# A dense gate matrix built with one 64-column matmul per token, the two halves of each gate added by VectorE, in one ring of 40 rows

## The chip, the cores and the metric

One core of one Trainium2 chip. The metric is the device time of one execution in microseconds; lower is better. The core has five engines that each run their own instructions in order: TensorE (PE; its weight loads are listed apart as PEld), VectorE (DVE), ScalarE (ACT), GpSimd (POOL) and SyncE (SP). They wait for each other with semaphores. Matmuls write into PSUM, which has banks of 128 x 512 float32; everything else lies in SBUF.

## The reference

The program is a trunk of two layers on 512 tokens of 1024 features. Layer 0 mixes tokens by windowed attention, layer 1 by a short gated convolution; each is followed by the same kind of expert layer, and that one takes nearly all the time:

```python
def peer_ffn(xn, w_query, sub_keys, expert_u, expert_v):
    q = (xt @ w_query).reshape(T, PEER_HEADS, 2, QUERY_HALF)
    s = jnp.einsum('thpd,hpnd->thpn', q, sub_keys)
    s_top, i_top = lax.top_k(s, PEER_TOPK)
    ...
    g_s, sel = lax.top_k(cand, PEER_TOPK)
    idx = jnp.take_along_axis(cand_idx, sel, axis=-1)
    g = jax.nn.softmax(g_s, axis=-1)
    ...
        u = jnp.take(expert_u, ic, axis=0)
        a = jnp.einsum('td,thkd->thk', xc, u)
        w = gc * jax.nn.gelu(a, approximate=False)
        v = jnp.take(expert_v, ic, axis=0)
        return jnp.einsum('thk,thkd->td', w, v)
```

So each token picks 8 x 16 = 128 experts out of 128 x 128 = 16384, each with a gate g. An expert is a row u and a row v of 1024 numbers; the token gets the sum of g * gelu(x . u) * v over its experts. An expert's number is 128 i + j, where i and j are its two keys.

## The kernel before

**Two ways for the tokens.** The 512 tokens are four tiles of 128. Tiles 0 and 1 are done by `gather` (L625): for each tile, 128 indirect loads fetch a row of u for each token (`ug`, L636, issued on GpSimd), and VectorE takes its dot product with the token (L639, a "dot" below, followed by a short read of the accumulator). Later 128 rows of v each are fetched (`vg`, L667) and multiplied on TensorE in pairs, eight matmuls of 512 columns to a pair (`acc`, L677).

Tiles 2 and 3, 256 tokens, are done by `dense` (L693): all 16384 experts are computed for all of them, and a gate matrix G that is zero almost everywhere picks. The loop runs over the 128 key blocks i, each with the 128 experts j. Its two halves are:

- `ustep(i)` (L704): the block of u is loaded, split into a rounded part (`uh`, cast on ScalarE, L701) and a remainder (`ul`, subtracted on VectorE, L702), and multiplied with the tokens in 24 matmuls of 256 columns into the bank psA (L178 to L183). ScalarE puts the gelu of it into `dw` (L712).
- `vstep(i)` (L715): `dw` is multiplied with the row of G for block i (L718; on VectorE, or on GpSimd while the gather's dots run), split into `wh` (ScalarE, L724) and `wl` (VectorE, L725); the block of v is split like u (`vh`, `vl`); 12 matmuls of 512 columns add to y (L736), which holds four banks from the first block to the last. `ustep` runs seven blocks ahead of `vstep` (LAG), and the first eight blocks' `dw` lie in a G tile not yet needed (`pre`).

**The gate matrix.** G[j, i, token] is the gate of expert (i, j). `gen(i, tg)` (L739) makes it for 32 blocks (a chunk) and 16 tokens (a group). VectorE builds three things in float16: `oj`, one where j is the expert's second key (128 x 2048, L745), `oi`, one where i is its first (128 x 512, L748), and two copies of `oi` times the gate, rounded and remainder (L751, twice; the gate is scaled by GSC). TensorE multiplies `oj` with them, for each token two matmuls of 32 columns that accumulate in the bank psG (L756, 32 matmuls in all). ScalarE scales the bank into four G tiles of eight rows each (L759). There are five such tiles, so 40 rows in flight. A layer has 4 chunks of 16 groups: 128 groups in the program. psG has one bank, which it shares by turns with other small products; psA has one as well.

**The order.** The code of `dense`, of the gather and of the next layer's front (mixer, router) is written as streams that a planner (`merge`) interleaves by estimated prices; in the loop, two groups for the next chunk are written before each vstep from the 25th of a chunk on (L782 to L787). The tile framework then schedules by simulated times; groups have a high priority (HPG), so they are taken as soon as their buffers and inputs are there. What comes out is a fixed order on each engine.

## Time and profile before

| | us |
|---|---|
| median of 3 runs | 3108.2 (3102.3 to 3110.3) |
| profiled execution, its own time | 3084.04 |
| its span, first to last instruction | 3082.2 |
| mean granted TensorE clock | 0.950 |
| dense loop of layer 0, first y matmul to the last chunk's end | 665 to 1670 |
| dense loop of layer 1 | 2117 to 3082 |

The chances in the prediction are about the median. The profile is of one execution, which was 0.8% under it. In the profile "busy" is the time in which an engine executes; matmuls are pipelined, so a TensorE that is busy all the time need not be at its peak. In the tables of windows each line is one stretch of the span: its length, then busy time and number of instructions of TensorE, its weight loads, VectorE, ScalarE and GpSimd, then the granted clock of TensorE as a share of 2.4 GHz, the share of the DMA engines in use, and the rate in GB/s.

### The profile page before, as it was taken

What the parts mean: (1) busy time and instruction counts of PE and PEld (TensorE: products, weight loads), DVE (VectorE), ACT (ScalarE), POOL (GpSimd) and SP (SyncE); (2) the same over time, 40 slices, a digit from 0 to 9 for tenths busy, and PEclk for the clock granted to TensorE, in tenths of its full rate; (3) what the DMA queues carried; (4) which work ended last, traced back from release to release, by engine and by line L of the source; (5) the groups of instructions that cost most, each with busy time, mean ns of one, the idle gap of its engine ahead of it and who ended that gap; (6) DMA issues with size and microseconds to landing.
All of it is one profiled execution on the core that took longest, in us unless ns stands there. A gap on an engine that the chain in (4) does not pass through costs nothing.

```text
span 3082.2 us, 53493 instructions
## 1 busy us (share of the span) xinstructions
PE 2782.4 (90%) x19980; PEld 2242.6 (73%) x19980; DVE 2255.1 (73%) x5363; ACT 1178.1 (38%) x2414; POOL 1352.1 (44%) x1154
## 2 busy tenths in 40 slices
PE   5964799999998999999997798999998798999998
PEld 5862367757986887778776787775787687778776
DVE  2499859887996997455459998887479999456444
ACT  4225433424333334344343334333434333334433
POOL 0157643354354444531347752345326866531331
PEclk8986899979999999999999899997999999999999
DMA  5888888879889977985999996787959988975996
GB/s 193 299 312 307 323 303 292 307 278 359 299 329 381 356 268 260 328 301 178 350 335 387 373 359 220 264 306 270 319 193 377 357 297 321 340 274 182 341 338 215
DMA packets 263205, 931.40 MB, mean 302 GB/s; under 512 B 29984, under 2 KB 38560, under 8 KB 262944
## 3 DMA queue, kind: packets, MB, share of 16 engines
q0 software_dynamic: 147456, 536.94, 48.1%
q1 hardware_dynamic: 115488, 391.03, 35.2%
q8 instruction: 158, 2.59, 0.3%
q14 instruction: 103, 0.84, 0.1%
HBM read 916.31 MB, written 11.53 MB: 301 GB/s over the span
## 4 chain that ended last, share of the span: by engine, by line
PE 72%; DVE 14%; DMA 5%; issue 4%; ACT 3%; POOL 1%; SPq 0%; DVEq 0%; ACTq 0%; POOLq 0%
PE y L736 20%; PE acc L677 9%; PE psG L756 9%; PE psA L180 8%; PE psA L181 7%; PE psA L183 7%; DVE ug L639 7%; PE psrq L568 3%; DMA ug<-in_u_dram,idx 2%; PE psbcu L404 1%; DMA vg<-in_v_dram,idxT 1%; PE psq L241 1%; DVE vl L702 1%; PE psrs L574 1%; PE psrq L180 1%
## 5 line engine op out<-in xcount | busy, mean ns | idle before, releaser
L667 POOL DMA_INDIRECT vg<-in_v_dram,idxT x512 | 550.0, 1074 | 945.7 <-PE acc L677 839.0
L636 POOL DMA_INDIRECT ug<-in_u_dram,idx x512 | 670.3, 1309 | 626.5 <-DVE act L639 269.8
L639 DVE CUSTOM_DVE_ANT_0 ug<-ug,xn 128x1024 f32<-128x1024 f32 x512 | 628.8, 1240 | 27.5 <-DMA ug<-in_u_dram,idx 26.7
L180 PE MATMUL psA<-xh,uh 128*128 128x256 f32 x2048 | 525.5, 294 | 44.7 <-ACT uh L701 26.8
L702 DVE TENSOR_TENSOR ul<-du,uh 128x1024 fp32r<-128x1024 f32 x256 | 316.4, 1236 | 264.5 <-ACT uh L701 244.9
L181 PE MATMUL psA<-xl,uh 128*128 128x256 f32 x2048 | 503.7, 284 | 0.0
L180 PEld LDWEIGHTS psA<-xh,uh 128*128 128x128 f32 x2048 | 391.9, 191 | 147.6 <-ACT wh L724 54.5
L702 DVE TENSOR_TENSOR vl<-dv,vh 128x1024 fp32r<-128x1024 f32 x256 | 319.9, 1249 | 183.5 <-ACT vh L701 169.4
L701 ACT CAST uh<-du 128x1024 fp32r<-128x1024 f32 x256 | 269.5, 1053 | 340.7 <-PE psA L181 296.4
L181 PEld LDWEIGHTS psA<-xl,uh 128*128 128x128 f32 x2048 | 391.5, 191 | 5.3 <-issue 3.0
L701 ACT CAST vh<-dv 128x1024 fp32r<-128x1024 f32 x256 | 268.8, 1051 | 240.8 <-PE y L736 198.3
L677 PE MATMUL acc<-vg,wd 128*32 128x512 f32 x2048 | 315.8, 637 | 10.4 <-DMA vg<-in_v_dram,idxT 10.0
L756 PEld LDWEIGHTS <-oj 128*128 128x128 f16 x4096 | 278.1, 159 | 63.1 <-issue 37.6
L736 PE MATMUL y<-vh,wh 128*128 128x512 f32 x1024 | 291.5, 404 | 26.6 <-ACT vh L701 26.6
L756 PE MATMUL psG<-oi,oj 128*128 128x32 f16 x4096 | 298.4, 249 | 7.6 <-ACT G L759 6.6
L183 PE MATMUL psA<-xh,ul 128*128 128x256 f32 x2048 | 292.2, 284 | 5.3 <-DVE ul L702 5.3
L736 PE MATMUL y<-vl,wh 128*128 128x512 f32 x1024 | 281.7, 397 | 11.6 <-DVE vl L702 11.6
L183 PEld LDWEIGHTS psA<-xh,ul 128*128 128x128 f32 x2048 | 264.4, 190 | 23.5 <-issue 9.2
L736 PE MATMUL y<-vh,wl 128*128 128x512 f32 x1024 | 278.7, 394 | 0.0
L759 ACT ACTIVATE G<-psG 128x128 f32<-128x128 f32 x512 | 102.5, 282 | 366.5 <-PE psG L756 346.2
L745 DVE TENSOR_TENSOR oj<-ijT,iorep 128x2048 f16<-128x2048 f16 x128 | 157.8, 1233 | 108.9 <-PE psG L756 108.6
L736 PEld LDWEIGHTS y<-vh,wh 128*128 128x128 f32 x1024 | 181.1, 192 | 71.4 <-ACT vh L701 35.1
(207 smaller groups left out, 3902.6 us busy)
## 6 DMA issues: line engine op xcount, KB each, us to landing
du<-in_uT_dram SPq DMA_DIRECT2D x256, 512.0 KB, 6.2
dv<-in_v_dram SPq DMA_DIRECT2D x256, 512.0 KB, 6.2
wpc<-in_wq_dram SPq DMA_DIRECT2D x64, 512.0 KB, 5.7
wpc<-in_w_in_dram SPq DMA_DIRECT2D x48, 512.0 KB, 6.7
wpo<-in_wo_dram SPq DMA_DIRECT2D x16, 512.0 KB, 4.5
ug<-in_u_dram,idx POOLq DMA_INDIRECT x512, 7.3
vg<-in_v_dram,idxT POOLq DMA_INDIRECT x512, 6.9
wpo<-in_w_out_dram SPq DMA_DIRECT2D x16, 512.0 KB, 7.3
```

The lines of the kernel that those rows point to most:

```text
L180: nc.tensor.matmul(ps, w[0][:, k, :], x[0][:, k, ts], start=(k == 0), stop=False)
L181: nc.tensor.matmul(ps, w[0][:, k, :], x[1][:, k, ts], start=False, stop=False)
L183: nc.tensor.matmul(ps, w[1][:, k, :], x[0][:, k, ts], start=False, stop=(k == KC - 1))
L636: nc.gpsimd.indirect_dma_start(out=ug, out_offset=None, in_=a[f"u{l}"], in_offset=bass.IndirectOffsetOnAxis(ap=r["idx"][h][:, c:c + 1], ax ...
L639: nc.vector.tensor_tensor_reduce(out=ug, in0=ug, in1=xn, scale=1.0, scalar=0.0, op0=ALU.mult, op1=ALU.add, accum_out=act[:, s:s + 1])
L667: ld = nc.gpsimd.indirect_dma_start(out=vg, out_offset=None, in_=a[f"v{l}"], in_offset=bass.IndirectOffsetOnAxis(ap=idxT[:, tt:tt + 1], ax ...
L677: mm = nc.tensor.matmul(acc[c:c + 32, :], wd[:, j, r8, :], vgs[j][:, h * 512:(h + 1) * 512], start=(q == 0 and r8 == 0), stop=(q == 3 and ...
L701: nc.scalar.copy(hi, w)
L702: nc.vector.tensor_tensor(lo, w, hi, op=ALU.subtract)
L736: nc.tensor.matmul(ys[tt][h], x[:, tt * P:(tt + 1) * P], m[:, h * 512:(h + 1) * 512], start=first and k == 0, stop=last and k == len(terms ...
L745: nc.vector.tensor_tensor(oj, jT.unsqueeze(1).to_broadcast([P, P, TG]), iorep, op=ALU.is_equal)
L756: nc.tensor.matmul(ps[:, T * IC:(T + 1) * IC], oj[:, :, T], oi[:, q, :, T], start=(q == 0), stop=(q == 1))
```

## The change

Three things are changed together, all in `dense`:

- The rounded gate and the remainder of one token are no longer two matmuls that accumulate. One matmul of 64 columns puts them side by side in psG. A bank then holds 8 tokens (TP) instead of 16, so each group has two parts of 8 matmuls.
- ScalarE scales the rounded half into G, and VectorE then adds the scaled remainder, read from PSUM (`scalar_tensor_tensor`, a new instruction).
- G is one tile, a ring of 40 rows (GR), in place of five tiles of 8 rows. The 32 rows of a chunk begin at row 0, 32, 24 or 16; where they run over the ring's end, both the scaling and the addition are split in two (8+24, 16+16 and 24+8 rows). The first eight `dw` lie in rows 32 to 39.

```diff
-HC = 8
+TP = 8
...
-GB = 5
+GR = 40
...
-            w = (pre[:, i, :] if i < npre else
+            w = (G[:, IC + i, :] if i < npre else
...
-            (nc.gpsimd if (WPU if st.get("gu") else WPV) else nc.vector).tensor_tensor(w, w, G[i // HC][:, i % HC, :], op=ALU.mult)
+            (nc.gpsimd if (WPU if st.get("gu") else WPV) else nc.vector).tensor_tensor(w, w, G[:, i % GR, :], op=ALU.mult)
...
-            ps = pmm("psG")
-            for T in range(TG):
-                for q in range(2):
-                    nc.tensor.matmul(ps[:, T * IC:(T + 1) * IC], oj[:, :, T], oi[:, q, :, T],
-                                     start=(q == 0), stop=(q == 1))
-            for hf in range(IC // HC):
-                nc.scalar.mul(G[i // HC + hf][:, :, tg * TG:(tg + 1) * TG],
-                              ps.rearrange("p (t i) -> p i t", i=IC)[:, hf * HC:(hf + 1) * HC, :], 1.0 / GSC)
+            for part in range(TG // TP):
+                ps = pmm("psG")
+                for T in range(TP):
+                    nc.tensor.matmul(ps[:, T * 2 * IC:(T + 1) * 2 * IC].rearrange("p (q i) -> p q i", q=2),
+                                     oj[:, :, part * TP + T], oi[:, 0:2, :, part * TP + T], start=True, stop=True)
+                psv = ps.rearrange("p (t q i) -> p q i t", q=2, i=IC)
+                tok = slice(tg * TG + part * TP, tg * TG + (part + 1) * TP)
+                r0 = i % GR
+                cut = min(IC, GR - r0)
+                for o, n, row in ((0, cut, r0), (cut, IC - cut, 0)):
+                    if n:
+                        g = G[:, row:row + n, tok]
+                        nc.scalar.mul(g, psv[:, 0, o:o + n, :], 1.0 / GSC)
+                        nc.vector.scalar_tensor_tensor(g, psv[:, 1, o:o + n, :], 1.0 / GSC, g,
+                                                       op0=ALU.mult, op1=ALU.add)
...
-        G = {}
+        G = pool.tile([P, GR, T2], F32, name="G")
...
-            if tg == 0:
-                for hf in range(IC // HC):
-                    G[c * (IC // HC) + hf] = pool.tile([P, HC, T2], F32, name="G", tag="G", bufs=GB)
...
-        npre = HC * PRE
-        pre = pool.tile([P, HC, T2], F32, name="pre", tag="G", bufs=GB) if PRE else None
+        npre = GR - IC
```

In numbers: 2048 matmuls in place of 4096 for G, 448 scalings in place of 512, and 448 new additions on VectorE. In the code after, the lines of `gen` are one lower up to the matmul (`oj` L744, `oi` L747 and L750, psG L755), the scaling is L764, the addition L765; ustep and vstep are one lower too.

The change also moves instructions. The places are the last chunk's gate matrix in layer 1 and the one of layer 0.

VectorE in layer 1, where the groups for the last chunk are made. Before, one group's `oj` and `oi` stand between the subtractions of a step:

```order
L725 TENSOR_TENSOR wl<-dw,wh 128x256
L745 TENSOR_TENSOR oj<-ijT,iorep 128x2048
L748 TENSOR_TENSOR oi<-ijT,iorep 128x512
L751 TENSOR_TENSOR oi<-oi,gb 128x512 x2
L702 TENSOR_TENSOR ul<-du,uh 128x1024
L718 TENSOR_TENSOR dw<-dw,G 128x256
L702 TENSOR_TENSOR vl<-dv,vh 128x1024
```

After, this piece of VectorE's order is part of a block in which it repeats about ten times with nothing of a step between:

```order
L744 TENSOR_TENSOR oj<-ijT,iorep 128x2048
L747 TENSOR_TENSOR oi<-ijT,iorep 128x512
L765 SCALAR_TENSOR_TENSOR G<-psG,G 128x24x8
L750 TENSOR_TENSOR oi<-oi,gb 128x512 x2
L765 SCALAR_TENSOR_TENSOR G<-psG,G 128x8x8
L765 SCALAR_TENSOR_TENSOR G<-psG,G 128x24x8
L765 SCALAR_TENSOR_TENSOR G<-psG,G 128x8x8
L744 TENSOR_TENSOR oj<-ijT,iorep 128x2048
```

The first two additions belong to the group before, part one; the next two to its part two. The `ul`, `dw`, `vl` and `wl` rows that stood between the groups stand before and behind the block.

ScalarE at the same place, before (the scalings of a group are four instructions, and the casts of the steps lie between):

```order
L759 ACTIVATE G<-psG 128x8x16 x4
L701 CAST uh<-du 128x1024
L712 ACTIVATE dw<-psA 128x256
L759 ACTIVATE G<-psG 128x8x16 x4
L701 CAST vh<-dv 128x1024
L724 CAST wh<-dw 128x256
```

and after, at the beginning of the block:

```order
L700 CAST vh<-dv 128x1024
L711 ACTIVATE dw<-psA 128x256
L764 ACTIVATE G<-psG 128x24x8
L764 ACTIVATE G<-psG 128x8x8
L764 ACTIVATE G<-psG 128x24x8
L764 ACTIVATE G<-psG 128x8x8
L764 ACTIVATE G<-psG 128x24x8
```

Over thirty scalings follow each other there; the next cast stands behind them. On TensorE the matmuls of 22 parts stand there behind each other in the same way, ahead of the last four vsteps of the chunk.

VectorE in layer 0 at the step to its last chunk, before (one step's work repeats; `wd` is a copy for the gather):

```order
L660 COPY wd<-wT 128x2x8
L702 TENSOR_TENSOR vl<-dv,vh 128x1024
L725 TENSOR_TENSOR wl<-dw,wh 128x256
L702 TENSOR_TENSOR ul<-du,uh 128x1024
L718 TENSOR_TENSOR dw<-dw,G 128x256
L702 TENSOR_TENSOR vl<-dv,vh 128x1024
L725 TENSOR_TENSOR wl<-dw,wh 128x256
```

After, the end of the block there, in which the gather's dots (two rows each, the second reads the accumulator) stand between the additions:

```order
L765 SCALAR_TENSOR_TENSOR G<-psG,G 128x24x8
L638 ISA ug,act<-ug,xn 128x1024
L638 ISA act 128x1
L638 ISA ug,act<-ug,xn 128x1024
L638 ISA act 128x1
L750 TENSOR_TENSOR oi<-oi,gb 128x512 x2
L765 SCALAR_TENSOR_TENSOR G<-psG,G 128x8x8
L638 ISA ug,act<-ug,xn 128x1024
L638 ISA act 128x1
L765 SCALAR_TENSOR_TENSOR G<-psG,G 128x24x8
L765 SCALAR_TENSOR_TENSOR G<-psG,G 128x8x8
```

Dots and gate parts that were spread over the steps have moved into this block, 67 dots in all.

Counted by vsteps (y groups of 12 matmuls on TensorE, `wl` on VectorE), the order holds this. A stretch is named by its first and last vstep, layer 1 going on from 128; gates are groups of 16 tokens before and parts of 8 tokens after, pairs are the gather's on TensorE.

| stretch | before: pairs, gates, dots | after: pairs, gates, dots |
|---|---|---|
| 0 to 28 | 11, 16, 49 | 0, 21, 75 |
| 28 to 32 | 0, 0, 12 | 0, 10, 30 |
| 32 to 60 | 8, 16, 67 | 25, 13, 23 |
| 60 to 64 | 5, 0, 0 | 19, 20, 0 |
| 64 to 92 | 27, 15, 0 | 20, 8, 31 |
| 92 to 96 | 6, 0, 0 | 0, 23, 67 |
| 96 to 124 | 18, 0, 32 | 0, 0, 0 |
| 124 to 128 and between the layers | 40, 17, 96 | 64, 33, 40 |
| 128 to 156 | 24, 16, 8 | 0, 10, 78 |
| 156 to 160 | 0, 0, 16 | 10, 21, 40 |
| 160 to 188 | 0, 13, 94 | 35, 13, 0 |
| 188 to 192 | 3, 3, 10 | 19, 20, 0 |
| 192 to 220 | 26, 15, 0 | 0, 9, 0 |
| 220 to 224 | 5, 0, 0 | 0, 22, 0 |
| 224 to the end | 30, 0, 0 | 0, 0, 0 |

## Rows read from the trace of the kernel before

**Rows 1.** The page's first part: engine, busy us, share of the span, instructions.

```profile
PE 2782.4 (90%) x19980; PEld 2242.6 (73%) x19980; DVE 2255.1 (73%) x5363; ACT 1178.1 (38%) x2414; POOL 1352.1 (44%) x1154
```

**Rows 2.** The page's fourth part: the chain that ended last, by engine.

```profile
PE 72%; DVE 14%; DMA 5%; issue 4%; ACT 3%; POOL 1%; SPq 0%; DVEq 0%; ACTq 0%; POOLq 0%
```

**Rows 3.** Windows of the eight long stretches: first, last, sum (columns as told above).

```profile
665.15:888.60 223.45, 213.93 (x1653) 182.11 (x1650) 190.64 (x367) 90.53 (x185) 95.87 (x77) 0.99 0.88 322
...
2877.06:3082.19 205.13, 193.09 (x1202) 144.37 (x1200) 89.94 (x117) 75.94 (x114) 54.67 (x56) 0.98 0.80 287
sum 1782.12, PE 1693.88 PEld 1380.45 DVE 1226.93 ACT 694.92 POOL 750.15; mean PE 211.74 PEld 172.56 DVE 153.37 ACT 86.87 POOL 93.77
```

**Rows 4.** Windows of the six short stretches of four vsteps: first, last, sum.

```profile
888.60:923.16 34.56, 33.13 (x236) 30.32 (x234) 32.39 (x57) 11.80 (x20) 23.77 (x18) 1.00 0.97 363
...
2849.47:2877.06 27.59, 27.59 (x185) 21.14 (x183) 12.70 (x17) 13.16 (x21) 10.09 (x11) 1.00 1.01 386
sum 187.51, PE 177.23 PEld 143.12 DVE 138.67 ACT 72.13 POOL 107.91; mean PE 29.54 PEld 23.85 DVE 23.11 ACT 12.02 POOL 17.98
```

**Rows 5.** Windows ahead of the first dense loop, and between the layers' loops.

```profile
0.00:665.15 665.15, 519.84 (x3713) 394.04 (x3713) 489.66 (x1809) 251.99 (x646) 279.41 (x250) 0.87 0.82 289
1670.06:2117.47 447.41, 391.48 (x2784) 325.01 (x2782) 399.88 (x1261) 159.08 (x323) 214.63 (x177) 0.91 0.83 300
```

**Rows 6.** The page's groups: busy us, mean ns, idle before and its releaser.

```profile
L639 DVE CUSTOM_DVE_ANT_0 ug<-ug,xn 128x1024 f32<-128x1024 f32 x512 | 628.8, 1240 | 27.5 <-DMA ug<-in_u_dram,idx 26.7
L702 DVE TENSOR_TENSOR ul<-du,uh 128x1024 fp32r<-128x1024 f32 x256 | 316.4, 1236 | 264.5 <-ACT uh L701 244.9
...
L756 PE MATMUL psG<-oi,oj 128*128 128x32 f16 x4096 | 298.4, 249 | 7.6 <-ACT G L759 6.6
...
L759 ACT ACTIVATE G<-psG 128x128 f32<-128x128 f32 x512 | 102.5, 282 | 366.5 <-PE psG L756 346.2
L745 DVE TENSOR_TENSOR oj<-ijT,iorep 128x2048 f16<-128x2048 f16 x128 | 157.8, 1233 | 108.9 <-PE psG L756 108.6
```

**Rows 7.** Further groups on VectorE, shapes kept apart.

```profile
L725 DVE TENSOR_TENSOR wl<-dw,wh 128x256 fp32r<-128x256 f32 x240 | 103.8, 432 | 11.5 <-ACT wh L724 11.2
L751 DVE TENSOR_TENSOR oi<-oi,gb 128x512 f16<-128x512 f16 x256 | 98.2, 425 | 1.2
L434 DVE MAX8 v<-rsc 128x8 f32<-128x128 f32 x256 | 61.2, 282 | 23.5 <-ACT rsc L577 23.4
L748 DVE TENSOR_TENSOR oi<-ijT,iorep 128x512 f16<-128x512 f16 x128 | 55.1, 431 | 0.0
L639 DVE DVE_READ_ACCUMULATOR2_ANT act<- 128x1 f32 x512 | 41.5, 81 | 0.0
```

**Rows 8.** The attention's mask step, VectorE reading PSUM, by size.

```profile
L317 DVE CUSTOM_DVE_ANT_0 sc<-psc,mask 128x256 f32<-128x256 f32 x48 | 17.9, 417 | 0.0
L317 DVE CUSTOM_DVE_ANT_0 sc<-psc,mask 128x128 f32<-128x128 f32 x16 | 3.8, 287 | 5.3 <-PE psc L311 5.3
```

**Rows 9.** Windows of two gate groups, at the lower and the full clock.

```profile
643.75:646.06 2.31, 2.31 (x40) 2.22 (x40) 1.51 (x6) 0.00 (x0) 2.01 (x2) 0.50 0.75 216
1366.19:1368.47 2.28, 2.28 (x37) 2.28 (x34) 0.85 (x2) 0.00 (x0) 1.64 (x2) 1.00 0.83 268
```

**Rows 10.** The chain in order of time (start, us): y groups of neighbouring steps.

```profile
1248.80 2.72 PE y L736 x12
...
1255.56 2.72 PE y L736 x12
...
1631.57 2.73 PE y L736 x12
...
1637.14 2.78 PE y L736 x12
```

**Rows 11.** The timeline of TensorE at the loop's start (start, us, idle before).

```profile
643.75 2.31 PE L756 MATMUL psG<-oi,oj 128*128 128x32 f16 x32
...
647.86 2.31 PE L756 MATMUL psG<-oi,oj 128*128 128x32 f16 x32
...
665.15 1.66 PE L736 MATMUL y<-vh,wh 128*128 128x512 f32 x4
```

More of the change, by code (lines that the diff above doesn't have):

```diff
@@ L55 @@
 DEC = 2
-PRE = 1
 FD1 = 80.0
@@ L717, in vstep @@
             w = ws.pop(i)
-            (nc.gpsimd if (WPU if st.get("gu") else WPV) else nc.vector).tensor_tensor(w, w, G[i // HC][:, i % HC, :], op=ALU.mult)
-            f = VU if st.get("gu") else VG if i % IC >= 2 * IC - GB * HC else VB0
+            (nc.gpsimd if (WPU if st.get("gu") else WPV) else nc.vector).tensor_tensor(w, w, G[:, i % GR, :], op=ALU.mult)
+            f = VU if st.get("gu") else VG if i % IC >= 2 * IC - GR else VB0
             sp = int((i + 1) * f) > int(i * f)
@@ L781, in dense @@
             c, q = divmod(i, IC)
-            q0 = 2 * IC - GB * HC
+            q0 = 2 * IC - GR
             if q >= q0 and c + 1 < NK // IC:
```

## The prediction

> **What bounds the kernel now.** I read the busy times first: TensorE is busy 2782 of 3082 us, VectorE 2255, no other engine over half [rows 1]. The chain that ended last is 72% TensorE and 14% VectorE [rows 2]. So a us taken from TensorE is worth nearly a us where TensorE is full, and nothing where VectorE is late. Which holds where, I read by stage. I cut the two dense loops at their vsteps: eight long stretches of 28 or 32 vsteps and six short ones of 4, the short ones being the last four of a chunk of 32. The long ones last 1782 us with TensorE busy in 95% [rows 3], the short ones 187.5 us, also 95% [rows 4]. Before them come 665 us and between the layers 447 us, where VectorE is nearly as busy as TensorE or busier [rows 5]. A short stretch costs hardly more than its four steps: a step without extra work takes 5.57 us between two y groups, one with two gathered blocks 6.76, so such a pair costs 1.2 [rows 10]. A y group is 2.73, which leaves 2.84 for psA. These three prices and 2.3 for a gate group rebuild the long stretch at 1241.88 (28 steps, 27 pairs, 15 gate groups) as 156 + 32 + 34 = 222 where it took 221.55. TensorE's sum is the bound there, and the gate groups are in it in full.
>
> **What the change takes from TensorE.** A gate group of 32 matmuls with 32 columns takes 2.31 us at a granted clock of 0.50 (1.2 GHz) and 2.28 at 1.00 (2.4 GHz) [rows 9]: 0.071 us each at either level, so columns don't set it. 128 groups are 294 us. Afterwards there are half as many matmuls, each twice as wide. Lower bound: the same 0.071 each, 0.57 a part of 8, 146 us for 256 parts. Upper bound: time by columns, 0.142 each, 291 us, no gain. I take the lower one, since the two clock levels show no dependence on the rate of columns, and 0.8 where a part stands among other work (0.57 and the change of bank and weights, an estimate): 205 us. TensorE gets 90 to 148 us less to do.
>
> **What it adds to VectorE and ScalarE.** There are 448 new operations of VectorE that read PSUM. Its mask step from PSUM takes 0.287 us for 128 elements and 0.417 for 256 [rows 8]. Hence 64 instructions of 32x8 rows at 0.42, and 384 of 24x8, 16x8 or 8x8 at 0.35, 0.287 and 0.22 (on the line through the two, an estimate), 0.285 in the mean: 27 + 109 = 136 us. They take no other operation away, so they can't cost less than nothing. As an upper bound a 24x8 and an 8x8, 0.57 together, take what two of 256 elements take, 0.84, if the scattered ring rows set the pace: 192 pairs, 52 us more. ScalarE's 512 multiplications [rows 6] become 448 of twice the elements in the mean, and it has 60% of the span free: nothing.
>
> **What it moves.** This decides. In the order before, the 16 gate groups of the next chunk lie half a vstep to one vstep apart, and most end some six vsteps before the chunk does. In the new order each engine takes about one part per vstep from the middle of the chunk, and 20 to 23 of the 32 parts are left for the short stretch (10 for chunk 1 of layer 0). There they stand on all three engines in one block with no y or psA between them. Order on an engine is kept, so the y and psA matmuls behind them wait, the casts wait on ScalarE, and the ul and vl subtractions on VectorE.
>
> How long is such a block? For 16 tokens VectorE does oj 1.23, oi 0.43, two oi 0.85 [rows 6, 7] and four additions of 1.14: 3.65 us. There is one bank for psG. The matmuls of a first part run beside the next oj; those of the second can only start when the first part's last addition has read the bank, and nothing is left to VectorE then: 0.57 of matmuls and 0.35 of ScalarE (24x8 elements, between rows 0.28 and 0.42) are added, 4.6 us in all. The trace of before has gate groups behind each other only with pairs between them, 4.1 us from start to start [rows 11], so that handover is nowhere bare in it; bounds are 3.65 (all hidden) and 5.5 (both parts bare). The Trainium skill, Perfetto Trace Analysis, section Optimizing Tensor Performance, says that "Independent matmul groups should rotate through different PSUM banks" so that the evacuation of one overlaps the next. By it the bare block would go at 3.65 with a second bank, some 30 us less over the three bare blocks; with one bank it speaks for 4.6, and no run here shows it yet.
>
> Short stretches, new. Three have no dots: four steps 22, plus 10 to 11 groups of 16 tokens at 4.6 (48), less 4 to 5 at the ends beside y: 66, 66, 65; the 19 pairs that two of them hold lie beside VectorE on TensorE. Three are filled with dots of the gather, and VectorE's sum sets them. A dot takes 1.24 and its accumulator read 0.08, 1.32 [rows 6]. Layer 0, chunk 3: 67 dots 88, ten groups 25, additions 14, twelve ul and vl 15 [rows 6], less 7 for overlap: 135. Layer 0, chunk 1: 30 dots 40, six groups 15, additions 7, thirteen ul and vl 16, some 145 short operations of the routing at an estimated 0.2 (its max takes 0.28 [rows 7]) 29: 105 after overlap. Layer 1, chunk 1: 40 dots 53, twelve groups 30, additions 13, ul and vl 16: 112. Sum 549, against 187.5: **+361**.
>
> Long stretches, new. They lose what the short ones took: 24 pairs fewer in all, gate parts, dots. By TensorE's sum (2.73, 2.84, 1.2, 0.8) and 3 to 5% of gaps: layer 0, chunk 1: 193, so 203; chunk 2: 183, so 192; chunk 3 (no pair, no gate) 142, so 148; layer 1: 205, so 207; 160, so 164; the last 152 and 15 to the end, 167. Two are VectorE's: the first of layer 0 (75 dots 99, 45 ul and vl 56, 28 wl and 17 dw 19 [rows 7], ten groups 25, additions 11, convolution and rest 19) 229, so 235; the first of layer 1 with 78 dots 193, 192. Sum 1508, against 1782: **-274**.
>
> Start of layer 0: 26 parts behind the last psA, 13 groups at 4.6 = 60, where nine groups of 32 matmuls stood, five of which took 21.4 us with their pairs, 4.3 each [rows 11] = 38: **+22**. Between the layers: 56 dots fewer take 74 from VectorE and 40 additions give 17 back, so TensorE bounds it: 391 [rows 5], less 17 groups of 2.3, plus 33 parts 26 and 24 pairs 29: 407, 417 with its gaps: **-30**. After each block TensorE starts at the lower level: the first four y matmuls behind the start took 1.66 us against 0.91 [rows 10, 11]; six blocks at 1.5 us: **+9**.
>
> Sum: 361 - 274 + 22 - 30 + 9 = +88. The profiled execution took 3084.0 us around its span of 3082.2; with 88 it is 3172. The median of the runs, 3108.2, is 0.8% above the profiled one, and the same ratio gives 3197; I say 3195.
>
> **Rivals.**
> Faster, VectorE never waits inside a block, because the next part's matmuls always find the bank read. Then bare blocks go at VectorE's 3.65 (-34), the filled ones lose what waits their sums hold (-15), the start loses nothing (-22), TensorE is held too shortly to fall to the lower level (-9), and the front, freed of dots, follows VectorE's sum by 80 instead of 30 (-50): +88 becomes -42, some 3066. The sign turns where more than 88 of these 130 come in. For it: VectorE is idle in a quarter of the span [rows 1]. Against: the one bank, and the 1508 count already what is freed.
> No change: only the dots and the start pay back so (the front -50, the start -22, no clock loss -9), with blocks as forecast: +7, 3115. For it: the front's two engines are about equally busy [rows 5]. Against: pairs have moved into it.
> Slower still, matmuls timed by their columns: a part 1.37 instead of 0.8, 146 us more on TensorE, an estimated 110 of it where it bounds: 3308. For it: no row holds a matmul of 64 columns with these weights. Against: 32 columns took the same at both levels [rows 9].
> That the change doesn't do what it says: the addition could be hidden and the parts spread as before; then only the 90 to 148 us come off, 2960 to 3020. The order excludes the spreading.
>
> **How the numbers follow.** Forecast 0.73; faster 0.13, nearly all by the first rival; no change 0.07; columns 0.07. Within the forecast the handover at 3.65 to 5.5 gives -34 to +30, slower ring writes +50, and the pace of dots (1.2 to 1.7 us) another 40 either way. The range is 3105 to 3285: it takes in the no-change rival, leaves out the faster one and most of the column one. About 0.3% is what a measurement of this kernel tells from no change: faster (under 3099) 0.13, same 0.07, slower (over 3117.5) 0.80.
>
> **What would show it.** Right: short stretches of 60 to 70 us without dots and 100 to 135 with them, TensorE idle there on psG with a releaser of line 765; long stretches at 1.5 ms in sum; a part's eight matmuls at 0.6 us. Wrong: short stretches under 45 us; parts at 1.1 us or more; additions over 0.4 us; a front that falls by 60 us or more.

## The result

The kernel after takes 3358.6 us in the median (3357.3 to 3359.8), before 3105.2 beside it. The ratio is 1.0816 (1.0795 to 1.0837): 8.2% slower, where 3195 (2.8%) was forecast and 3285 was the range's upper end. The side was right, the size three times too small. The profiled execution took 3357.3 us around a span of 3355.5, 273 us more than the span before; the forecast stood at +88. Some 21 of the 273 are not the change's: the profile before is of an execution of 3084.0 us, and the runs beside the result took 3105.2. By medians it is +253 against +87.

### The profile page after: what moved, and what is told of

Read it like the earlier page. It is cut to its first block, busy times and chain, and to the rows that moved or that the text cites. A ratio compares the mean times of both kernels' runs of the same rounds, so it can differ in the third digit from the quotient of the medians.

```text
span 3355.5 us, 49790 instructions
## 1 busy us (share of the span) xinstructions
PE 2827.2 (84%) x17932; PEld 2230.8 (66%) x17932; DVE 2352.6 (70%) x5811; ACT 1204.3 (36%) x2351; POOL 1341.2 (40%) x1154
## 5 line engine op out<-in xcount | busy, mean ns | idle before, releaser
L635 POOL DMA_INDIRECT ug<-in_u_dram,idx x512 | 657.6, 1284 | 692.8 <-DVE act L638 262.9
L666 POOL DMA_INDIRECT vg<-in_v_dram,idxT x512 | 559.3, 1092 | 708.6 <-PE acc L676 598.7
L638 DVE CUSTOM_DVE_ANT_0 ug<-ug,xn 128x1024 f32<-128x1024 f32 x512 | 621.2, 1227 | 54.5 <-DMA ug<-in_u_dram,idx 46.6
L179 PE MATMUL psA<-xh,uh 128*128 128x256 f32 x2048 | 516.5, 290 | 22.5 <-ACT G L711 9.3
L755 PE MATMUL psG<-oi,oj 128*128 128x64 f16 x2048 | 304.8, 308 | 229.7 <-DVE G L765 226.1
L755 PEld LDWEIGHTS <-oj 128*128 128x128 f16 x2048 | 242.2, 151 | 380.5 <-DVE G L765 245.4
L676 PE MATMUL acc<-vg,wd 128*32 128x512 f32 x2048 | 348.2, 716 | 19.1 <-DMA vg<-in_v_dram,idxT 17.5
L764 ACT ACTIVATE G<-psG 128x64 f32<-128x64 f32 (+3 forms) x448 | 130.7, 292 | 635.3 <-PE psG L755 426.3
L735 PE MATMUL y<-vh,wl 128*128 128x512 f32 x1024 | 288.6, 405 | 22.0 <-DVE wl L724 21.9
L735 PEld LDWEIGHTS y<-vh,wl 128*128 128x128 f32 x1024 | 197.8, 195 | 73.4 <-DVE wl L724 28.1
```

Source lines behind the costliest of these rows:

```text
L179: nc.tensor.matmul(ps, w[0][:, k, :], x[0][:, k, ts], start=(k == 0), stop=False)
L635: nc.gpsimd.indirect_dma_start(out=ug, out_offset=None, in_=a[f"u{l}"], in_offset=bass.IndirectOffsetOnAxis(ap=r["idx"][h][:, c:c + 1], ax ...
L638: nc.vector.tensor_tensor_reduce(out=ug, in0=ug, in1=xn, scale=1.0, scalar=0.0, op0=ALU.mult, op1=ALU.add, accum_out=act[:, s:s + 1])
L666: ld = nc.gpsimd.indirect_dma_start(out=vg, out_offset=None, in_=a[f"v{l}"], in_offset=bass.IndirectOffsetOnAxis(ap=idxT[:, tt:tt + 1], ax ...
L676: mm = nc.tensor.matmul(acc[c:c + 32, :], wd[:, j, r8, :], vgs[j][:, h * 512:(h + 1) * 512], start=(q == 0 and r8 == 0), stop=(q == 3 and ...
L735: nc.tensor.matmul(ys[tt][h], x[:, tt * P:(tt + 1) * P], m[:, h * 512:(h + 1) * 512], start=first and k == 0, stop=last and k == len(terms ...
```

## The profile after

The page's first part; it answers to [rows 1]:

```profile
PE 2827.2 (84%) x17932; PEld 2230.8 (66%) x17932; DVE 2352.6 (70%) x5811; ACT 1204.3 (36%) x2351; POOL 1341.2 (40%) x1154
```

TensorE executes 2048 instructions fewer and is busy 45 us longer; 32 of the 45 are the gather's pairs (`acc`, 348.2 us where it was 315.8), of which more ran at the lower clock. So the first expectation, 90 to 148 us less, failed at once. The groups of the gate matrix, from the page and from the list with shapes kept apart (columns as in [rows 6, 7]):

```profile
L755 PE MATMUL psG<-oi,oj 128*128 128x64 f16 x2048 | 304.8, 308 | 229.7 <-DVE G L765 226.1
```

```profile
L765 DVE SCALAR_TENSOR_TENSOR G<-psG,G 128x192 f32<-128x192 f32 x128 | 45.2, 353 | 29.2 <-ACT G L764 29.1
L765 DVE SCALAR_TENSOR_TENSOR G<-psG,G 128x128 f32<-128x128 f32 x128 | 36.8, 287 | 74.7 <-ACT G L764 58.0 <-issue 16.7
L765 DVE SCALAR_TENSOR_TENSOR G<-psG,G 128x64 f32<-128x64 f32 x128 | 28.3, 221 | 16.9 <-ACT G L764 13.0 <-issue 3.9
L765 DVE SCALAR_TENSOR_TENSOR G<-psG,G 128x256 f32<-128x256 f32 x64 | 27.0, 422 | 11.4 <-ACT G L764 9.9 <-issue 1.6
```

Half the matmuls take 304.8 us where twice as many took 298.4 [rows 6], and TensorE now sits idle 229.7 us ahead of them, nearly all of it for the addition of line 765; before it was 7.6. The additions themselves cost what was forecast: 0.353, 0.287, 0.221 and 0.422 us, 137 us in all against 136.

The windows of the long stretches (vsteps 0 to 28, and so on; columns as in [rows 3]) and of the short ones [rows 4], and the start and front, cut at the same vsteps:

```profile
699.50:954.05 254.55, 238.73 (x1569) 208.88 (x1565) 220.47 (x452) 95.67 (x185) 111.71 (x82) 0.98 0.95 356
...
3186.59:3355.50 168.91, 156.31 (x936) 138.76 (x936) 89.42 (x121) 71.62 (x107) 0.00 (x0) 0.95 0.49 165
sum 1555.49, PE 1481.72 PEld 1237.03 DVE 1040.87 ACT 633.89 POOL 578.08; mean PE 185.22 PEld 154.63 DVE 130.11 ACT 79.24 POOL 72.26
```

```profile
954.05:1038.34 84.29, 56.03 (x415) 51.36 (x413) 83.14 (x285) 26.13 (x65) 28.03 (x27) 0.84 0.81 281
1258.27:1353.68 95.41, 74.80 (x482) 45.41 (x481) 51.39 (x94) 25.65 (x62) 48.31 (x49) 0.80 0.78 273
1551.97:1688.78 136.81, 55.22 (x353) 46.65 (x353) 120.27 (x231) 26.00 (x67) 85.47 (x66) 0.62 0.85 301
2524.99:2637.27 112.28, 70.52 (x418) 46.70 (x418) 91.55 (x181) 24.64 (x65) 67.21 (x58) 0.67 0.89 313
2846.89:2935.54 88.65, 75.73 (x482) 45.58 (x481) 45.09 (x92) 25.42 (x62) 36.46 (x37) 0.81 0.76 266
3100.84:3186.59 85.75, 51.21 (x347) 43.66 (x345) 44.38 (x94) 24.99 (x64) 0.00 (x0) 0.70 0.21 67
sum 603.19, PE 383.51 PEld 279.35 DVE 435.82 ACT 152.83 POOL 265.49; mean PE 63.92 PEld 46.56 DVE 72.64 ACT 25.47 POOL 44.25
```

The six short stretches hold the loss: 603 us where there were 187.5, TensorE busy in 64% instead of 95%. The long ones give back 227 (1555 against 1782). In the last short stretch every engine is idle for long: VectorE is busy 44 of 86 us, TensorE 51, ScalarE 25, GpSimd 0. That is a chain of handovers, not a full engine. Its timeline, one group of 16 tokens (start and duration in us, behind the row the idle time before it and its releaser):

```profile
3150.32 1.20 PE L755 MATMUL psG<-oi,oj 128*128 128x64 f16 x8 [2.73 <-DVE G L765]
3151.55 0.33 ACT L764 ACTIVATE G<-psG 128x192 f32<-128x192 f32 x1 [1.83 <-PE psG L755]
3151.91 0.36 DVE L765 SCALAR_TENSOR_TENSOR G<-psG,G 128x192 f32<-128x192 f32 x1 [1.65 <-ACT G L764]
3152.31 0.22 ACT L764 ACTIVATE G<-psG 128x64 f32<-128x64 f32 x1 [0.42 <-DVE G L765]
3152.56 0.23 DVE L765 SCALAR_TENSOR_TENSOR G<-psG,G 128x64 f32<-128x64 f32 x1 [0.29 <-ACT G L764]
3152.85 1.19 PE L755 MATMUL psG<-oi,oj 128*128 128x64 f16 x8 [1.33 <-DVE G L765]
3154.07 0.33 ACT L764 ACTIVATE G<-psG 128x192 f32<-128x192 f32 x1 [1.54 <-PE psG L755]
3154.07 1.22 DVE L744 TENSOR_TENSOR oj<-ijT,iorep 128x2048 f16<-128x2048 f16 x1 [1.28 <-PE psG L755]
3155.22 0.42 DVE L747 TENSOR_TENSOR oi<-ijT,iorep 128x512 f16<-128x512 f16 x1
3155.55 0.35 DVE L765 SCALAR_TENSOR_TENSOR G<-psG,G 128x192 f32<-128x192 f32 x1
3155.82 0.75 DVE L750 TENSOR_TENSOR oi<-oi,gb 128x512 f16<-128x512 f16 x2
3155.94 0.22 ACT L764 ACTIVATE G<-psG 128x64 f32<-128x64 f32 x1 [1.53 <-DVE G L765]
3156.49 0.22 DVE L765 SCALAR_TENSOR_TENSOR G<-psG,G 128x64 f32<-128x64 f32 x1
3156.76 1.20 PE L755 MATMUL psG<-oi,oj 128*128 128x64 f16 x8 [2.72 <-DVE G L765]
```

Read it as one thread: at hardly any time are two of the three engines at work. Eight matmuls take 1.20 us, not 0.57. Scaling and addition go by turns, since the second scaling also waits for the first addition (0.42 us, released by line 765). Behind the first part TensorE waits 1.33 us for that. Behind the second it waits 2.72, because `oj`, `oi` and the two multiplications stand ahead of the last addition on VectorE. From 3150.32 to 3156.76 a group takes 6.44 us; the prediction had 4.6.

TensorE at the start of layer 1's loop, where parts and pairs alternate (same columns):

```profile
2249.36 1.94 PE L676 MATMUL acc<-vg,wd 128*32 128x512 f32 x8
2251.99 1.14 PE L755 MATMUL psG<-oi,oj 128*128 128x64 f16 x8 [0.69 <-DVE G L765]
2253.06 1.94 PE L676 MATMUL acc<-vg,wd 128*32 128x512 f32 x8
2254.93 1.20 PE L755 MATMUL psG<-oi,oj 128*128 128x64 f16 x8
```

And the windows of that place and of the start of layer 0, followed by the two of before that answer to them:

```profile
2250.00:2333.27 83.27, 57.54 (x337) 26.54 (x330) 62.58 (x172) 15.55 (x35) 56.60 (x51) 0.58 0.85 291
620.00:699.50 79.50, 66.76 (x369) 29.08 (x368) 60.71 (x220) 15.92 (x37) 48.26 (x44) 0.56 0.84 283
```

```profile
2070.00:2117.47 47.47, 42.55 (x423) 25.52 (x421) 39.79 (x152) 14.44 (x54) 21.93 (x21) 0.60 0.73 252
625.00:665.15 40.15, 38.66 (x351) 21.16 (x349) 31.96 (x121) 10.34 (x41) 18.80 (x19) 0.50 0.73 252
```

A pair that takes 1.06 us at the full clock (in the stretch from 2637.27, at 0.99) takes 1.94 here, and a part goes with it each time: some 3.1 us a part where nothing waits, at a granted clock of 0.56 and 0.58. The two windows hold 23 and 25 parts, 3.6 and 3.2 us each; those of before hold 10.5 and 8.7 groups (335 and 278 matmuls in the records), 4.5 and 4.6 us a group or 2.3 for as many tokens as a part has, at much the same clock.

All of the time between the layers (the sum over 1835.95 to 2333.27; the second line of [rows 5] is before's):

```profile
sum 497.32, PE 423.09 PEld 322.43 DVE 364.23 ACT 164.26 POOL 192.89; mean PE 47.01 PEld 35.83 DVE 40.47 ACT 18.25 POOL 21.43
```

TensorE is busy 423 of 497 us there, 391 of 447 before: its idle time grew from 56 to 74 us.

## The experiments

The theory after the first profile: each half of the change costs for itself. The matmul of 64 columns saves nothing, because its columns lie 32 bytes apart; and the addition puts VectorE between the one bank and the next part, which collects the parts in blocks and makes each block a bare chain. The rivals: it is VectorE's 137 us of work; it is the ring, to whose one tile all users and writers are tied; it is the doubled matmul.

All ratios are against the kernel before on the same chip. It took 3085 us on two of the chips used and 3106 to 3108 on a third, so times of different experiments are compared by ratio.

**Neighbouring columns.** The same 64 columns are read side by side; the gate matrix then holds other numbers.

```diff
-  ps[...].rearrange("p (q i) -> p q i", q=2), oj[:, :, part * TP + T], oi[:, 0:2, :, part * TP + T]
+  ps[...].rearrange("p (a b) -> p a b", a=4), oj[:, :, part * TP + T], oi[:, T % 2, 4 * part:4 * part + 4, :]
```

> The kernel after, but the 64 columns of each gate matmul are read as 64 neighbouring float16 numbers, not every 16th one. The gate matrix holds other numbers then; number, order and size of the instructions stay the same up to four rows. In the profile of the kernel after, a part of eight took 1.19 us at either clock level, 0.130 a matmul. Theory A (the moving columns are read at about 2 ns each because neighbours lie 32 bytes apart): a part falls to 0.8 us or less, 0.06 to 0.08 a matmul; 256 parts save about 120 us on TensorE, most of it exposed in the blocks: 3230 to 3270 us. Rival B (64 columns cost 0.13 however they lie, or the weights' layout sets it): a part stays at 1.19 and the time at 3350 to 3365.

Measured: 3288.4 us, ratio 1.0585 (1.0553 to 1.0617). In the last block:

```profile
3098.11 0.71 PE L755 MATMUL psG<-oi,oj 128*128 128x64 f16 x8 [2.73 <-DVE G L765]
3100.15 0.70 PE L755 MATMUL psG<-oi,oj 128*128 128x64 f16 x8 [1.33 <-DVE G L765]
3103.58 0.71 PE L755 MATMUL psG<-oi,oj 128*128 128x64 f16 x8 [2.73 <-DVE G L765]
```

A part falls from 1.19 to 0.70 us with the same weights in the same places, and a bare group from 6.44 to 5.47, just twice that. So the price of the doubled matmul is the layout of its columns; rival B falls. From the start of one matmul to that of the next it is 0.127 us with the stride and 0.062 without (medians over both traces). Of the 125 us of parts (256 x 0.49) 70 come off, fewer than the expected 90 to 130, and the time lies above theory A's range. Cut at the same vsteps, the long stretches give 35 of the 70, the short ones 27, the start 9, the time between the layers nothing. Why it is fewer was not measured; an engine that ends later than TensorE in those places would explain it. The waits of 2.73 and 1.33 us are untouched.

**No addition.** The line of VectorE's addition is taken out, so the remainder of each gate is missing in G.

```diff
-  nc.vector.scalar_tensor_tensor(g, psv[:, 1, o:o + n, :], 1.0 / GSC, g, op0=ALU.mult, op1=ALU.add)
```

> The kernel after without VectorE's 448 additions: the remainder is computed but left out of the gate matrix. The order then has 2, 3, 11, 11, 8 and 11 parts in the six short stretches where it had 10, 20, 23, 21, 20 and 22. Theory A (the blocks and their length come from the addition, which puts VectorE between a part's matmuls and the next part): most of the loss goes, 3120 to 3180 us. Rival B (the doubled matmul is the main loss, the addition a minor one of 136 us of VectorE time that is partly hidden): 3260 to 3320 us.

Measured: 3132.6 us, 1.0085 (1.0054 to 1.0117). Theory A: 226 us of the loss go with 137 us of work, more than the work itself. The short stretches come to 259 us in sum (31 to 55 each).

**The ring alone**, with the old matmuls, in groups of 16 tokens and split scalings; and **the ring with halved parts**, two matmuls of 32 columns a token.

```diff
-  nc.tensor.matmul(<64 columns>, start=True, stop=True)
+  for q in range(2):
+      nc.tensor.matmul(ps[:, T * IC:(T + 1) * IC], oj[:, :, ...], oi[:, q, :, ...], start=(q == 0), stop=(q == 1))
...
-  nc.vector.scalar_tensor_tensor(...)
```

(TP is 16 in the first and 8 in the second.)

> Only the ring of the change: G is one tile of 40 rows with split scalings, but a group is 32 matmuls of 32 columns for 16 tokens that accumulate, as before, with no addition. Theory A (the ring does nothing): the order of the gate groups is that of before, 3090 to 3120 us, within 0.5% of before. Rival B (one tile makes every user of G wait for every writer): short stretches of 35 us and more, over 3140 us.

> Ring and halved parts, but each token's two halves are two matmuls of 32 columns that accumulate, as before, and there is no addition: a part is 16 matmuls for 8 tokens in half a bank. It differs from the run without the addition only in 16 matmuls of 32 columns in place of 8 of 64. Theory A (TensorE's price goes by columns, 16 x 0.071 = 1.14 against 8 x 0.130 = 1.04 to 1.19): the same as that run within 1%, 3120 to 3180 us, by the halved parts some 30 us over before. Rival B (a matmul costs the same at 32 and 64 columns in a free stretch): some 80 to 140 us slower than that run.

Measured: 3151.1 us, 1.0140 (1.0108 to 1.0173), and 3166.4 us, 1.0188 (1.0156 to 1.0219). The first met neither theory: the gate groups stand as before and the short stretches are not long (28 to 42 us), yet it is 1.4% slower. The second lies at the edge of theory A's 1%: the kernel without addition is 1.0% faster, with a part of 1.19 us against 1.27, so the one matmul of 64 columns does gain something by itself: half the matmuls bring 1.0 point. Rival B's 80 to 140 us are out. From the second kernel, at the end of its last block:

```profile
2962.45 1.27 PE L756 MATMUL psG<-oi,oj 128*128 128x32 f16 x16
```

Where the ring alone loses, shown by the windows of its last long stretch and of about the first of layer 1, which lies at 2136.70 to 2360.49 [rows 3 has the last one of before, 205.13 us]:

```profile
2923.40:3151.90 228.50, 217.34 (x1250) 146.49 (x1249) 90.09 (x118) 78.91 (x118) 67.14 (x69) 0.99 0.83 289
2132.00:2355.00 223.00, 220.03 (x1565) 160.09 (x1564) 128.80 (x231) 78.82 (x135) 56.78 (x54) 0.98 0.67 231
```

These two stretches (205.13 and 206.22 us before) hold 40 of the 70 us by which its profiled span exceeds that of before (some 21 of the 70 are the faster execution in the profile before), with 36 instead of 30 pairs in the last one. So either one tile or another order of the gather could be the reason.

**The ring with four scalings.** As the ring alone, but with the four scalings of eight rows that the kernel before has; they never run over the ring's end.

```diff
-  for o, n, row in ((0, cut, r0), (cut, IC - cut, 0)):
+  for o, n, row in [(o, 8, (i + o) % GR) for o in range(0, IC, 8)]:
```

> Matmuls, group size and four scalings of eight rows as before; the five tiles of G are one ring of 40 rows. Row for row the order on TensorE is that of before. The ring with two longer scalings took 1.014 of before. Theory A (the one tile costs nothing; the 1.4% came from the order that the scheduler found for the other scalings): 0.997 to 1.003 of before. Rival B (one tile adds waits): 1.010 to 1.018.

Measured: 1.0005 (0.9993 to 1.0016). Theory A: the one tile costs nothing, and rival B falls. The 1.4% go with the different scalings, and with them the scheduler came to another interleaving, in which more pairs are left for the end. That the interleaving costs the 1.4% is read from the two windows; why the scheduler chose it was not tried.

**The remainder copied out by ScalarE.** VectorE still makes its 448 additions, but from SBUF; the bank is free when ScalarE is through.

```diff
+  lo = pool.tile([P, IC, TP], F32, name="lo", tag="glo", bufs=2)
+  nc.scalar.mul(lo, psv[:, 1], 1.0 / GSC)
...
-  nc.vector.scalar_tensor_tensor(g, psv[:, 1, o:o + n, :], 1.0 / GSC, g, op0=ALU.mult, op1=ALU.add)
+  nc.vector.tensor_tensor(g, g, lo[:, o:o + n, :], op=ALU.add)
```

> The kernel after, but ScalarE also copies the scaled remainder out of PSUM (one instruction of 32x8 more a part, 256 in all, 0.38 us each = 97 us of ScalarE), and VectorE's 448 additions read it from SBUF. VectorE keeps its additions; the bank is free when ScalarE is through. In the order 3, 8, 12, 9, 13 and 12 parts stand in the short stretches (after: 10, 20, 23, 21, 20, 22). Theory A (the addition costs by holding the one bank until VectorE comes to it): most of the 226 us between the kernel after and the run without additions go, 3140 to 3200 us. Rival B (it costs by VectorE's 136 us of work): 3280 to 3350 us.

Measured: 3173.2 us, 1.0296 (1.0273 to 1.0318). Its additions take VectorE as long as in the kernel after, and ScalarE has 98 us more:

```profile
L760 ACT ACTIVATE lo<-psG 128x256 f32<-128x256 f32 x256 | 98.5, 385 | 433.5 <-PE psG L755 425.6 <-DVE act L638 2.5 <-DVE oj L744 2.3
L767 DVE TENSOR_TENSOR G<-G,lo 128x192 f32<-128x192 f32 x128 | 45.3, 354 | 37.9 <-ACT G L766 37.8
```

In its last block parts follow each other thus:

```profile
2991.86 1.17 PE L755 MATMUL psG<-oi,oj 128*128 128x64 f16 x8
...
2993.34 0.44 ACT L766 ACTIVATE G<-psG 128x192 f32<-128x192 f32 x2
2993.70 0.49 DVE L767 TENSOR_TENSOR G<-G,lo 128x192 f32<-128x192 f32 x2
2993.84 1.15 PE L755 MATMUL psG<-oi,oj 128*128 128x64 f16 x8 [0.81 <-ACT G L766]
...
2995.80 1.16 PE L755 MATMUL psG<-oi,oj 128*128 128x64 f16 x8 [0.81 <-ACT G L766]
```

1.97 us from part to part, 3.9 a group in place of 6.44, and only 8 to 13 parts in five of the blocks, 3 in the first. ScalarE's two scalings now follow each other without a wait for the first addition, though the ring is the same one tile. So it was the common bank, not the ring, that made scaling and addition take turns.

This is the run that decides: the same work on VectorE, out of the bank's handover, costs 2.1 percentage points over no addition (1.0296 against 1.0085); inside the handover it costs 7.3 (1.0816). At least 5.2 of the 7.3 points are the wait, not the work. What no run separates is how the 5.2 split between the shorter chain of a part and the order that the scheduler made with it (57 parts in the six blocks instead of 116), and whether the 2.1 are VectorE's work or ScalarE's 98 us.

**Two banks.** The second part of a group goes into the front stream's bank.

```diff
-  ps = pmm("psG")
+  ps = (pf if part else pmm)("psG")
```

> The kernel after, but the second part of each group goes into the bank of the front stream, so two banks take turns and the additions still read PSUM. In the order 17, 24, 14, 17, 8 and 11 parts stand in the short stretches. Theory A (handover of the one bank): the two bare parts of a group, 6.44 us apart from group to group in the kernel after, come to 4.5 to 5.2, and fewer stand in blocks: 3220 to 3300 us. Rival B (the blocks are set by oj and the order on VectorE, not by the bank): 3330 to 3370 us.

Measured: 3255.2 us, 1.0562 (1.0539 to 1.0585): in the direction of theory A, a third of the loss. The last two short stretches come to 36 and 40 us (after: 89 and 86), with 8 and 11 parts left in them instead of 20 and 22, and two parts of a group follow each other with four matmuls of a step between them and no idle time:

```profile
3059.41 1.19 PE L755 MATMUL psG<-oi,oj 128*128 128x64 f16 x8
...
3061.37 1.20 PE L755 MATMUL psG<-oi,oj 128*128 128x64 f16 x8
```

That is 1.96 us, where 2.53 to 3.9 lay between parts with one bank. A bare group, for which 4.5 to 5.2 us were expected, could not be read: no bare block is left. The other four stretches stay at 87 to 125 us: three hold 45 to 61 dots, and into the fourth have moved the next router's matmuls, whose bank it is that is borrowed. So a second bank helped in the two stretches where nothing else is crowded in. The rule of the Trainium skill (Perfetto Trace Analysis, Optimizing Tensor Performance) that independent matmul groups should rotate through different PSUM banks agrees with these two stretches (36 and 40 us for 89 and 86) and was no cure for the other four.

**Three buffers for oj**, and then **for oj and oi**.

```diff
-  oj = pool.tile([P, P, TG], F16, name="oj", tag="oj", bufs=2)
+  oj = pool.tile([P, P, TG], F16, name="oj", tag="oj", bufs=3)
...
-  w = ... name="dw", tag="dw", bufs=LAG + 2
+  w = ... name="dw", tag="dw", bufs=LAG + 1
```

(In the second run `oi` has three buffers too, `dw` keeps its own, and WPB is 3 instead of 4.)

> The kernel after with three buffers for oj (and one dw buffer less, for the room). In a bare block of the kernel after, oj waits for the last matmul of a part and then stands ahead of the additions that free the bank. With a third buffer oj can run beside that part's matmuls. The order has as many parts in the blocks as after. Theory A (this wait is a piece of the 6.44 us a group): 5.0 to 5.6 us a bare group and 1.055 to 1.072 of before (after: 1.0816). Rival B (the bank alone sets it): 6.3 to 6.5 us and 1.078 to 1.085.

> The kernel after with three buffers for oj and for oi (with two of oi, the wait of oj only passed to oi and a bare group stayed at 6.44 us); for the room, the weight pieces of the other stages have three buffers instead of four, which touches only the front and the start. Blocks as after. Theory A (VectorE's oj and oi stand exposed in the handover because their buffers come free only with a part's last matmul): oj and oi (1.6 us) run beside a part's 1.2 us of matmuls, a bare group takes 5.2 to 5.4 us, and the time is 1.060 to 1.073 of before (after: 1.0816). Rival B (the order on VectorE and the one bank set it whatever the buffers): 6.3 to 6.5 us, 1.078 to 1.085.

Measured: 1.0802 (1.0776 to 1.0828) and 1.0811 (1.0783 to 1.0839). Both are rival B. From the second run, one group apart:

```profile
3155.55 1.22 PE L755 MATMUL psG<-oi,oj 128*128 128x64 f16 x8 [2.73 <-DVE G L765]
...
3158.09 1.20 PE L755 MATMUL psG<-oi,oj 128*128 128x64 f16 x8 [1.33 <-DVE G L765]
3159.33 1.23 DVE L744 TENSOR_TENSOR oj<-ijT,iorep 128x2048 f16<-128x2048 f16 x1 [1.29 <-PE psG L755]
...
3162.02 1.20 PE L755 MATMUL psG<-oi,oj 128*128 128x64 f16 x8 [2.73 <-DVE G L765]
```

6.47 us. `oj` still waits for a part's last matmul (1.29 us): with a further buffer VectorE only builds one group further ahead, until that buffer is taken too. A buffer can't shorten a chain whose slowest step empties the buffers. VectorE's order itself, with the next group's `oj` and `oi` ahead of the releasing additions, was changed alone in no run.

**The right layout of oi**, token by token, in the kernel after and in the kernel before.

```diff
-  oi = pool.tile([P, 3, IC, TG], F16, name="oi", tag="oi", bufs=2)
+  oi = pool.tile([P, TG, 3, IC], F16, name="oi", tag="oi", bufs=2)
...
-  nc.tensor.matmul(..., oj[:, :, part * TP + T], oi[:, 0:2, :, part * TP + T], ...)
+  nc.tensor.matmul(..., oj[:, :, part * TP + T], oi[:, part * TP + T, 0:2, :], ...)
```

> The kernel after with oi laid out token by token, so that the 64 columns of a matmul lie side by side with the right values in them; VectorE builds oi in that layout, with a broadcast in the innermost place. A part takes 0.70 us as in the run with neighbouring columns. 15, 19, 23, 23, 19 and 23 parts in the short stretches. If VectorE's oi costs what it did (0.43 and 0.85 a group): 3270 to 3300 us as that run. Rival: the broadcast makes the three instructions slower, 0.3 us each or more in a chain of 128 groups: 3310 to 3370 us.

> The kernel before with that layout of oi and nothing else changed: still two matmuls of 32 columns a token. If the price of a matmul goes by its strided columns, 0.071 us falls towards the spacing that remains for weights and issue, some 0.06, 4096 times: 20 to 45 us less, 3060 to 3090 us. Rival: 32 columns are already at the floor and VectorE's oi is slower: 3105 to 3140 us.

Measured: 3367.0 us, 1.0903 (1.0882 to 1.0924), and 3130.9 us, 1.0145 (1.0128 to 1.0162). Both go the rival's way and, by ratio, a little beyond its ranges (3310 to 3370 us are 1.066 to 1.085 of 3105, 3105 to 3140 are 1.000 to 1.011). From the kernel after with this layout, shapes kept apart (before: 425 and 431 ns [rows 7]):

```profile
L752 DVE TENSOR_TENSOR oi<-oi,gb 128x512 f16<-128x512 f16 x256 | 168.5, 698 | 0.0
L749 DVE TENSOR_TENSOR oi<-ijT,io 128x512 f16<-128x512 f16 x128 | 87.4, 683 | 0.0
```

In this layout (the broadcast innermost, the result in rows of 32 numbers with gaps; which of the two costs was not separated) each instruction takes some 0.26 us more, 0.8 a group, 100 us in all. That is the 3.2 points between this run and the one with neighbouring columns (1.0903 against 1.0585), and more than the 70 us that the shorter parts gave. In the kernel before, a group of 32 matmuls goes from 2.28 to 2.16 us, 15 us in all: at 32 columns there is little to gain from the layout.

**GpSimd adds** what ScalarE copied out.

```diff
-  nc.vector.tensor_tensor(g, g, lo[:, o:o + n, :], op=ALU.add)
+  nc.gpsimd.tensor_tensor(g, g, lo[:, o:o + n, :], op=ALU.add)
```

> As the run in which ScalarE copies the remainder out of PSUM (1.0296 of before), but GpSimd adds it, not VectorE. Blocks hold 0, 9, 12, 9, 13 and 12 parts. If what is left of the loss there was VectorE's 128 us of additions: 1.008 to 1.018 of before, near the run without additions (1.0085). If GpSimd's additions, of which a 128x256 product took 1.2 us in the kernel before, delay its indirect loads: 1.03 to 1.07.

Measured: 1.0379 (1.0354 to 1.0403), slower than with VectorE: 0.87 us on GpSimd for 128x192 where VectorE takes 0.354, 339 us in all, on the engine that issues the indirect loads. So the 1.008 to 1.018 that should have come if VectorE's additions were what was left did not come; it does not settle that question, since GpSimd's own price came in.

No version beat the kernel before. In a row, each one edit on (the first is from another chip than the rest): ring 1.0005, split scalings 1.014, halved parts 1.019, one matmul of 64 columns without the remainder 1.0085, the remainder added by VectorE out of PSUM 1.0816.

## Why the prediction was right and wrong

**Right.** That blocks form, where they stand, and that they outweigh what the long stretches give back. The additions' own price (137 us). The filled short stretches: 84, 137 and 112 us where 105, 135 and 112 were forecast. Six of the eight long ones within 4%.

**Wrong, in this order.** The miss is 273 - 88 = 185 us. Some 20 of it are the faster execution in the profile before and can't be put to one term; by medians it is 253 - 87 = 166.

- *The matmul's price.* The step was: the same time at both clock levels, so columns don't set it. That doesn't follow. It shows that TensorE's own clock doesn't set it; something that runs at its own pace beside that clock can still go by columns. It did: 1.19 us a part at either level, and 0.70 with neighbouring columns, near the 0.57 that I took. What the sum left out is the stride of the columns. Parts at 1.1 us or more, which the prediction named as a sign of being wrong, came. The rival that had the price right, by columns, got 0.07. The long stretches exceed 1508 by 47 us, and 35 of these go in the run with neighbouring columns (1520.8 in sum).
- *The bare group*, 4.6 us forecast, 6.44 measured, with an upper bound of 5.5 that was no bound. Two matmul prices of 0.62 too little are 1.24 of the 1.84. The rest, 0.6, is the step "the matmuls of a first part run beside the next oj": the order already showed that the additions of a group's last part stand behind the next group's `oj` and `oi`, so the bank is held through them and VectorE is idle during both parts' matmuls. The three bare stretches took 270 us instead of 197: 73.
- *The front*, -30 forecast, +50 measured: 80 us, the largest miss. Its sum took TensorE's work, 407 us, as the bound and gave it 10 us of gaps. The work came to 423, so 16 of the 80; the other 64 are idle time, 74 us. Nothing in the trace of before spoke for 10: TensorE was idle there for 447 - 391 = 56 us [rows 5], 36 of them for VectorE's normalized `h`, a wait of which 20 us were left after, though the dots had become fewer. 26 of the 74 lie in a block of its own at the front's end, like the one at the start of layer 0, which I had priced: 83 us at the lower clock instead of the 23 x 0.8 = 18 and some 19 pairs at 1.2 = 23 that the sum held.
- *The start*: 34 against 22, at 3.1 us a part with a pair in place of 2.3.
- The filled stretches came out 19 us shorter, and the 9 us for the clock after the blocks have no place of their own in the measured stretches. 73 + 47 + 80 + 12 - 19 - 9 = 184.

The rival by columns, 3308, came nearest, but in part by luck: it added the doubled price and left the overlap in the bare group and the gaps of the front as they were, so it is still low.

## What to carry to other kernels

Before a change puts a second engine between a PSUM bank and its next use, write down the chain of one handover and of everything queued ahead of the releasing instruction; where only one bank turns, that chain is the price, whatever the engines' busy shares. Free the bank with the engine that reads it first and do the arithmetic from SBUF; here that took the loss from 8.2% to 3.0%. Gaps that a trace shows on the engine that you take as the bound stay in the sum unless you can say what ends them. And a time that doesn't change with an engine's clock is not shown to be independent of the amount of work: vary the amount.

## What the runs showed of the hardware

- Eight matmuls with 64 float16 columns that lie 32 bytes apart took 1.14 to 1.20 us in stretches with a granted clock of 0.56 to 0.58 and 1.20 at 0.99; with the columns side by side 0.70. Thirty-two matmuls of 32 columns took 2.28 us with the stride and 2.16 without. Side by side, 64 columns cost no more than 32: 0.062 us from the start of one matmul to the next for both.
- A float16 operation of VectorE on 128x512 elements took 0.43 us with the broadcast operand's zero stride outermost, and 0.68 to 0.70 with it innermost and the result in rows of 32 numbers with gaps between them.
- GpSimd added 128x64 numbers in SBUF in 0.63 us and 128x192 in 0.87; VectorE took 0.22 and 0.35 for the same.
